# Hybrid encoder step on one core: one transfer for the rotary queries, and an order of instructions laid out by due times

## The chip, the cores and the metric

The kernel runs on one core of a Trainium2 chip. TensorE (PE) multiplies matrices, VectorE (DVE), ScalarE (ACT) and GpSimd (POOL) work on tiles, and SyncE (SP) issues every DMA of this kernel. Each engine runs its own list of instructions in a fixed order, and waits for the others by semaphores. The metric is the device time of one execution in microseconds (us), the median of several runs; less is better.

## What is computed

One step of a two-layer encoder: 2048 prompt rows (16 tiles of 128) and 64 sample rows (a 17th tile), 1024 columns. Each layer has one input projection, four groups of four heads, and one output projection:

```python
bi = branch_inputs(x, lp, jnp.arange(S))       # rms, x @ w_in, per-head rms
o_a = band_attn_prompt(bi['aq'], bi['ak'], bi['av'], lp['a_rel_bias'])
kb, vb = mla_keys(bi['ckv'], bi['krope'], lp)  # keys: 64 columns per head + 32 rotary ones
o_b = chunk_causal_attn_blocks(bi['bq'], kb, vb, MLA_SCALE)
o_c = stick_break_blocks(bi['cq'], bi['ck'], bi['cv'])
o_m = dense_attn(bi['mq'], mk, mv, HEAD_DIM ** -0.5)
y = merge(x, (o_a, o_b, o_c, o_m), bi['gates'], lp)   # rms per head, gate, @ w_out, + x
```

Group A looks at its own chunk and 8 before, B at the whole past, with a rotary part of 32 columns per head, C breaks a stick (a running product along the keys), M looks at 256 memory rows. Everything is float32.

## The kernel before

A float32 value is held as the sum of a rounded high part and a low part, and a product is made of several matmuls of such parts. For the rotary part of group B four row blocks of 32 are stacked to 128 rows: queries (high, low, high, high), keys (high, high, low, zero). `qr_stack` stores the query parts of a tile to DRAM, three blocks of them, and `load_q` reads them back for two tiles of one head, with four transfers into the tile `qr` [128 x 256], which has one buffer. `kr_stack` does the same for the keys by way of `ksbuf`.

The work is written as two streams of Python generators, which the loop at the end of `hybrid_step` interleaves. `p_stream` holds the projections: matmuls into `pp` (two PSUM banks of their own), weights split by POOL and DVE into `wh`, rows into `xh` and `xl`. `attention` goes through units, two query tiles by up to four key tiles: scores into `ps`, softmax or scan into `s` (`step`, `s1b`), transposes into `pt`, copies to `ph` (ACT the high part, DVE the low part, `s2`), the product into `ot` (`s3`), and its transpose into `ob`, from which ACT and DVE bring the result to `opark` (`s4`, `combine`). `ps`, `pt`, `ob` and all small transposes share five PSUM banks (`ps_st`). In group C a DVE scan (`TENSOR_TENSOR_SCAN` into `r`) makes the running product. `merge` normalises and gates the finished group.

What each generator issues is not sent to the engines at once. `Plan.add` records it with what it depends on, and `Plan.issue` lays all of it out in a modelled time: an operation becomes ready when the last one that it depends on has ended, plus a reserve that depends on the engine that receives it (`LAG`, in ns), and each engine that is free takes one of its ready operations, if the buffers that it opens are free in turn. Before, it takes the one that was recorded first. The order thus found is what each engine then runs; the modelled time itself is not used on the chip. Since one line (296) sends off every instruction, groups in the profile are told apart by the names of tiles.

Of the kernel before, what the change touches and what calls it, by code (L numbers as in the profile page):

```python
# [7 lines left out]
F32 = mybir.dt.float32  # L8
# [37 lines left out]
class Plan:  # L46
# [1 line left out]

    LAG = {"PE": 160, "DVE": 100, "ACT": 100, "POOL": 150, "SP": 200}

    def __init__(self):
        self.ops = []
# [129 lines left out]
    def issue(self, tc):  # L184
        import heapq
        ops, tiles = self.ops, self.tiles
        n = len(ops)
        after = [[] for _ in range(n)]
        left = [0] * n
        for i, op in enumerate(ops):  # L190
            left[i] = len(op[4])
            for j in op[4]:
                after[j].append(i)
        free, order, turn, uses = {}, {}, {}, {}
        for name, (key, k, count, bufs) in sorted(tiles.items(), key=lambda x: x[1][1]):
            free[key] = bufs
            order.setdefault(key, []).append(name)
            uses[name] = count
        rank = {x: i for names in order.values() for i, x in enumerate(names)}
        turn = {key: 0 for key in order}  # L200
        held = set()
        parked = {key: [] for key in order}
        ready = {e: [] for e in ("PE", "DVE", "ACT", "POOL", "SP")}
        clock = {e: 0.0 for e in ready}
        at = [0.0] * n
        start = [0.0] * n
        events, seq, act = [], 0, 0
        for i in range(n):
            if left[i] == 0:
                heapq.heappush(ready[ops[i][0]], i)  # L210

        def slot(i):

            for x in ops[i][5]:
                if x not in held:
                    key = tiles[x][0]
                    if free[key] <= 0 or order[key][turn[key]] != x:
                        return key
            return None

        now, done, wire = 0.0, 0, 0.0
        while done < n:
            moved = False
            for e in ready:
                while clock[e] <= now and ready[e]:
                    i = heapq.heappop(ready[e])
                    key = slot(i)
                    if key is not None:
                        parked[key].append(i)
                        continue  # L230
                    for x in ops[i][5]:
                        if x not in held:
                            k = tiles[x][0]
                            held.add(x)
                            free[k] -= 1
                            turn[k] += 1
                            if turn[k] < len(order[k]) and free[k] > 0:
                                for j in parked[k]:
                                    heapq.heappush(ready[ops[j][0]], j)
                                parked[k] = []  # L240
                    take, last = ops[i][6]
                    if e == "ACT":
                        t = self.table(ops[i][3])
                        if t and t != act:
                            act = t
                            take, last = take + 1300, last + 1300
                    if e == "SP":

                        begin = max(now + 2000, wire)
                        wire = begin + 0.004 * last  # L250
                        last = max(wire, now + 2000 + 0.0045 * last) - now + 300
                    start[i] = now
                    clock[e] = now + take
                    heapq.heappush(events, (now + take, 0, e, i))
                    heapq.heappush(events, (now + last, 1, e, i))
                    moved = True
                    break
            if moved:
                continue
            if not events:  # L260
                raise AssertionError(("plan", done, {k: (v[:3], [ops[j][0] for j in v[:3]]) for k, v in parked.items() if v}))
            now = events[0][0]
            while events and events[0][0] <= now:
                _, kind, e, i = heapq.heappop(events)
                if kind == 0:
                    if e == "PE":
                        for j in after[i]:
                            if ops[j][0] == "PE":
                                left[j] -= 1
                                if left[j] == 0:  # L270
                                    heapq.heappush(ready["PE"], j)
                    continue
                if kind == 1:
                    done += 1
                    for x in ops[i][5]:
                        uses[x] -= 1
                        if uses[x] == 0:
                            k = tiles[x][0]
                            held.discard(x)
                            free[k] += 1  # L280
                            for j in parked[k]:
                                heapq.heappush(ready[ops[j][0]], j)
                            parked[k] = []
                    for j in after[i]:
                        if e == "PE" and ops[j][0] == "PE":
                            continue
                        heapq.heappush(events, (now + (10 if ops[j][0] == e else self.LAG[ops[j][0]]), 2, e, j))
                    continue
                left[i] -= 1
                if left[i] == 0:  # L290
                    heapq.heappush(ready[ops[i][0]], i)
        self.span = now
        with tc.manual_schedule():
            for i in sorted(range(n), key=lambda i: (start[i], i)):
                op = ops[i]
                op[1](*op[2], **op[3])  # L296
# [21 lines left out]
def hybrid_step(  # L318
# [62 lines left out]
    G.memset(zrow, 0.0)  # L381
    for x in qbuf:
        V.tensor_copy(x[64:128, 1], zrow[64:128])
    ksbuf = [const.tile([128, 4, 32], F32R, name=f"ksbuf{i}") for i in range(2)]
    for x in ksbuf:
        V.tensor_copy(x[:, 3], zrow[:, 0:32])
    rot = {"q": 0, "ks": 0}

    def copy_r(dst, src):
# [15 lines left out]
    def layer_dram(l):  # L405
        d = {}
        for b, tl in enumerate(blocks):
            d["QR", b] = dt(f"qr{l}_{b}", [3, 128, len(tl) * 128])
            for g in "ABCM":
                d["Q" + g, b] = dt(f"q{g}{l}_{b}", [2, 256, len(tl) * 128])  # L410
                d["G" + g, b] = dt(f"g{g}{l}_{b}", [128, len(tl), 256])
        for g in "ABC":
            d["KV" + g] = dt(f"kv{g}{l}", [2, NH, HD, (NT + 3) // 4, 2, 512])
        for s in ("SA", "SB", "SC", "M", "SM"):
            d["KV" + s] = dt(f"kv{s}{l}", [2, NH, HD, 2, 256])
        d["KR"] = dt(f"kr{l}", [128, NT * 128])
        d["KRS"] = dt(f"krs{l}", [128, 256])
        d["Y"] = {t: dt(f"y{l}_{t}", [128, 1024]) for t in range(NT + 1)}
        D[l] = d
# [343 lines left out]
    def qr_stack(src, dst):  # L763

        pt = ps_st.tile([128, 128], F32, name="ptqr")
        T.transpose(pt, src, ident)
        kt = pj.tile([128, 2, 128], F32R, tag="qrs", name="qrs", bufs=1)
        A.copy(out=kt[:, 0], in_=pt)
        sub_r(kt[:, 1], pt, kt[:, 0])
        Y.dma_start(out=dst[0:2].rearrange("a p t -> p a t"), in_=kt.bitcast(F32))  # L770
        Y.dma_start(out=dst[2], in_=kt[:, 0].bitcast(F32))

    def v_stack(src, dst):

# [7 lines left out]
    def kr_stack(kr, dst):  # L782

        ks = ksbuf[rot["ks"] % 2]
        rot["ks"] += 1
        copy_r(ks[:, 0:2], kr.unsqueeze(1).to_broadcast([128, 2, 32]))
        sub_r(ks[:, 2], kr, ks[:, 0])
        yield
        pt = ps_st.tile([128, 128], F32, name="ptr")
        T.matmul(pt, lhsT=ks.rearrange("p a c -> p (a c)"), rhs=identr, start=True, stop=True)  # L790
# [4 lines left out]
    def small_T(src, n, tag):  # L795

        pt = ps_st.tile([128, n, 128], F32, name="pts")
        for k in range(n):
            T.transpose(pt[:, k, :], src[:, k * 128:(k + 1) * 128], ident)
        h = pj.tile([128, n, 128], F32R, tag=tag + "h", name=tag + "h", bufs=1)  # L800
        lo = pj.tile([128, n, 128], F32R, tag=tag + "l", name=tag + "l", bufs=1)
        A.copy(out=h, in_=pt)
        sub_r(lo, pt, h)
        return h, lo
# [582 lines left out]
    def group_units(l, b, g):  # L1387
# [13 lines left out]
        def load_q(p):  # L1401
# [4 lines left out]
            Y.dma_start(out=p["q"][0:64, :, 0:w].bitcast(F32), in_=src)  # L1406
            Y.dma_start(out=p["q"][64:128, 0, 0:w].bitcast(F32), in_=src[:, 0])
            if g == "B":
                p["qr"] = at.tile([128, 256], F32R, tag="qr", name="qr", bufs=1)
                for e in range(4):  # L1410
                    Y.dma_start(out=p["qr"][32 * e:32 * e + 32, 0:w].bitcast(F32),
                                      in_=d["QR", b][e % 3, h * 32:(h + 1) * 32, t0:t0 + w])

        for h in range(NH):
            start = []
# [409 lines left out]
```

## Time and profile before

| | us |
|---|---|
| median of 3 runs | 3259.86 (3255.87 to 3268.64) |
| the profiled execution's own time | 3260.81 |
| its span, first to last instruction | 3258.8 |
| PE busy | 3137.9 |
| PE loading weights | 3005.6 |
| DVE busy | 2684.0 |
| ACT busy | 1956.7 |
| POOL busy | 1509.6 |

The span is what the views of the profile divide up; the execution's own time is 2.0 us longer, and the median of the runs 0.95 us below that. PE's weight loads overlap its matmuls. SP is not in the busy times, since issuing a DMA is not counted; its issues are found in the timeline as SPq.

### The profile page before, as it was taken

What the parts mean: (1) busy time and instruction counts of PE and PEld (TensorE: products, weight loads), DVE (VectorE), ACT (ScalarE), POOL (GpSimd) and SP (SyncE); (2) the same over time, 40 slices, a digit from 0 to 9 for tenths busy, and PEclk for the clock granted to TensorE, in tenths of its full rate; (3) what the DMA queues carried; (4) which work ended last, traced back from release to release, by engine and by line L of the source; (5) the groups of instructions that cost most, each with busy time, mean ns of one, the idle gap of its engine ahead of it and who ended that gap; (6) DMA issues with size and microseconds to landing.
All of it is one profiled execution on the core that took longest, in us unless ns stands there. A gap on an engine that the chain in (4) does not pass through costs nothing. (4 is left out here: it accounts for less than half of the span.)

```text
span 3258.8 us, 75626 instructions
## 1 busy us (share of the span) xinstructions
PE 3137.9 (96%) x24486; PEld 3005.6 (92%) x24486; DVE 2684.0 (82%) x7977; ACT 1956.7 (60%) x5336; POOL 1509.6 (46%) x2353
## 2 busy tenths in 40 slices
PE   8999999999999999999999999999999999999899
PEld 7999889999999998999999889999999998998798
DVE  5687778998888789887877977899878888887984
ACT  4455656767665565565656765676646667665650
POOL 4655445665345246443434644466413544213562
PEclk9999999999999999999999999999999999999999
DMA  6755676644666766556566567754455776566545
GB/s 184 194 153 158 189 224 192 163 120 136 172 167 175 213 188 182 155 159 180 152 176 189 167 174 231 192 146 128 138 144 161 211 204 192 158 170 185 154 130 155
DMA packets 576123, 558.94 MB, mean 172 GB/s; under 512 B 70961, under 2 KB 478001, under 8 KB 575729
## 3 DMA queue, kind: packets, MB, share of 16 engines
q1 hardware_dynamic: 575728, 554.10, 60.2%
q8 instruction: 196, 3.21, 0.4%
q14 instruction: 199, 1.62, 0.2%
HBM read 378.21 MB, written 173.75 MB: 169 GB/s over the span
## 5 line engine op out<-in xcount | busy, mean ns | idle before, releaser
L296 PE MATMUL pp<-wh,xh 128*128 128x256 f32 (+1 forms) x9104 | 1804.6, 291 | 22.3 <-ACT ev L296 9.7
L296 PEld LDWEIGHTS pp<-wh,xh 128*128 128x128 f32 x9104 | 1436.3, 190 | 60.5 <-DVE wh L296 17.5
L296 PE MATMUL pp<-wh,xl 128*128 128x256 f32 (+1 forms) x4416 | 1238.2, 282 | 2.5 <-DVE xl L296 2.1
L296 PEld LDWEIGHTS pp<-wh,xl 128*128 128x128 f32 x4416 | 839.1, 190 | 7.8 <-DVE xl L296 4.5
L296 POOL TENSOR_SCALAR wh<-raw,gc 128x256 fp32r<-128x256 f32 (+1 forms) x848 | 467.5, 566 | 363.9 <-PE pp L296 268.1
L296 ACT CAST ph<-pt 128x512 fp32r<-128x512 f32 (+2 forms) x840 | 453.1, 550 | 283.5 <-PE pt L296 275.5
L296 DVE TENSOR_TENSOR ph<-pt,ph 128x512 fp32r<-128x512 f32 (+2 forms) x840 | 522.9, 633 | 119.2 <-ACT ph L296 116.0
L296 PE MATMUL ot<-ph,kv 128*128 128x256 f32 (+1 forms) x3232 | 579.3, 289 | 5.3 <-ACT os L296 1.7
L296 PE MATMUL ps<-kv,qbuf 128*128 128x256 f32 (+3 forms) x2048 | 543.4, 361 | 30.4 <-DVE r L296 8.5
L296 PE MATMUL pt<-identr,s 128*128 128x128 f32 x3056 | 504.4, 275 | 16.5 <-DVE r L296 4.8
L296 DVE SCALAR_TENSOR_TENSOR wh<-raw,gc,wh 128x256 fp32r<-128x256 f32 (+1 forms) x848 | 476.7, 597 | 22.1 <-POOL wh L296 21.5
L296 ACT ACTIVATE s<-s,nm 128x512 f32<-128x512 f32 (+4 forms) x600 | 384.3, 643 | 169.4 <-DVE nm L296 159.1
L296 PEld LDWEIGHTS ot<-ph,kv 128*128 128x128 f32 x3232 | 466.1, 190 | 18.8 <-DVE ph L296 4.4
L296 POOL TENSOR_TENSOR s<-s,r 128x512 f32<-128x512 f32 (+3 forms) x328 | 321.7, 983 | 245.0 <-DVE r L296 204.8
L296 POOL TENSOR_TENSOR st<-st,mhalf 128x4 f32<-128x4 f32 (+1 forms) x312 | 279.7, 902 | 246.1 <-DVE st L296 193.7
L296 PEld LDWEIGHTS pt<-identr,s 128*128 128x128 f32 x3056 | 356.6, 141 | 30.8 <-ACT s L296 6.6
L296 DVE TENSOR_TENSOR_SCAN r<-ps,r,one 128x512 f32<-128x512 f32 (+3 forms) x328 | 354.0, 1101 | 27.3 <-ACT ps L296 22.9
L296 PEld LDWEIGHTS ps<-kv,qbuf 128*128 128x128 f32 x2048 | 320.2, 190 | 58.2 <-DVE r L296 12.8
L296 ACT ACTIVATE ev<-pp,xst 128x256 f32<-128x256 f32 (+1 forms) x424 | 199.7, 472 | 264.0 <-PE pp L296 226.4
L296 POOL TENSOR_TENSOR mst<-mst,mhalf 128x4 f32<-128x4 f32 x136 | 138.9, 1026 | 252.9 <-DVE mst L296 244.1
L296 ACT ACTIVATE s<-ps 128x512 f32<-128x512 f32 (+3 forms) x328 | 166.4, 536 | 97.7 <-DVE ps L296 48.1
L296 DVE TENSOR_SCALAR_CACHE_REDUCE s<-ps 128x512 f32<-128x512 f32 (+1 forms) x328 | 181.6, 573 | 23.3 <-PE ps L296 22.7
(151 smaller groups left out, 4005.0 us busy)
## 6 DMA issues: line engine op xcount, KB each, us to landing
raw<-in_w_in SPq DMA_DIRECT2D x288, 256.0 KB, 3.4
kv<-kvC SPq DMA_DIRECT2D x128, 256.0 KB, 4.2
kv<-kvB SPq DMA_DIRECT2D x128, 256.0 KB, 4.2
kv<-kvA SPq DMA_DIRECT2D x96, 256.0 KB, 4.5
raw<-in_w_out SPq DMA_DIRECT2D x96, 256.0 KB, 3.7
y<-y SPq DMA_DIRECT2D x136, 128.0 KB, 2.7
xin<-y SPq DMA_DIRECT2D x64, 256.0 KB, 3.8
qC<-kt SPq DMA_DIRECT2D x34, 256.0 KB, 3.1
```

What stands on the lines that cost most here:

```text
L296: op[1](*op[2], **op[3])
```

## The change

`qr` is stored as four row blocks instead of three, the last two by one transfer from the same high part. It is read back by one transfer whose rows are interleaved: the four parts of a row lie next to each other on neighbouring partitions. The keys in `ksbuf` are interleaved in the same way. `qr` has two buffers; the two small transposes before low-rank products (`cT`, `qT`) share one pair of tiles, `sTh` and `sTl`.

In the planner, the reserves grow, and every operation gets a due time. An operation of PE or SP is due at the sum of PE's costs recorded ahead of it. One of DVE, ACT or POOL is due when its earliest reader is, less its own duration and 100 ns (and at most 100 us after its own place). A free PE takes the first recorded of those that have been ready for 300 ns, and if there is none, the first recorded. DVE and ACT take the one that is due first among those ready for 200 ns, or else among all; POOL and SP the one due first.

```diff
-    LAG = {"PE": 160, "DVE": 100, "ACT": 100, "POOL": 150, "SP": 200}
+    AGE = dict(PE=300,DVE=200,ACT=200,POOL=0,SP=0)
+    LAG = dict(PE=300,DVE=200,ACT=200,POOL=250,SP=300)
...
+        due, run = [0.0] * n, 0.0
+        for i, op in enumerate(ops):
+            due[i] = run
+            if op[0] == "PE":
+                run += op[6][0]
+        for i in range(n - 1, -1, -1):
+            if ops[i][0] in ("DVE","ACT","POOL"):
+                wait = 4000 if ops[i][0] == "SP" else ops[i][6][1] + 100
+                due[i] = min([due[i] + 100000] + [due[j] - wait for j in after[i]])
...
-                    i = heapq.heappop(ready[e])
+                    q = ready[e]
+                    if e == "PE":
+                        i = min((j for j in q if at[j] + self.AGE[e] <= now), default=q[0])
+                    else:
+                        i = min((j for j in q if at[j] + self.AGE[e] <= now), key=lambda j: due[j], default=None)
+                        if i is None:
+                            i = min(q, key=lambda j: due[j])
+                    q.remove(i)
+                    heapq.heapify(q)
...
                 if left[i] == 0:
+                    at[i] = now
                     heapq.heappush(ready[ops[i][0]], i)
...
-    ksbuf = [const.tile([128, 4, 32], F32R, name=f"ksbuf{i}") for i in range(2)]
+    ksbuf = [const.tile([128, 32, 4], F32R, name=f"ksbuf{i}") for i in range(2)]
...
-            d["QR", b] = dt(f"qr{l}_{b}", [3, 128, len(tl) * 128])
+            d["QR", b] = dt(f"qr{l}_{b}", [4, 128, len(tl) * 128])
...
-        Y.dma_start(out=dst[2], in_=kt[:, 0].bitcast(F32))
+        Y.dma_start(out=dst[2:4].rearrange("a p t -> p a t"),
+                          in_=kt[:, 0:1].bitcast(F32).to_broadcast([128, 2, 128]))
...
-        copy_r(ks[:, 0:2], kr.unsqueeze(1).to_broadcast([128, 2, 32]))
-        sub_r(ks[:, 2], kr, ks[:, 0])
+        copy_r(ks[:, :, 0:2], kr.unsqueeze(2).to_broadcast([128, 32, 2]))
+        sub_r(ks[:, :, 2], kr, ks[:, :, 0])
...
-        h = pj.tile([128, n, 128], F32R, tag=tag + "h", name=tag + "h", bufs=1)
-        lo = pj.tile([128, n, 128], F32R, tag=tag + "l", name=tag + "l", bufs=1)
+        h = pj.tile([128, n, 128], F32R, tag="sTh", name=tag + "h", bufs=1)
+        lo = pj.tile([128, n, 128], F32R, tag="sTl", name=tag + "l", bufs=1)
...
-                p["qr"] = at.tile([128, 256], F32R, tag="qr", name="qr", bufs=1)
-                for e in range(4):
-                    Y.dma_start(out=p["qr"][32 * e:32 * e + 32, 0:w].bitcast(F32),
-                                      in_=d["QR", b][e % 3, h * 32:(h + 1) * 32, t0:t0 + w])
+                p["qr"] = at.tile([128, 256], F32R, tag="qr", name="qr", bufs=2)
+
+                Y.dma_start(out=p["qr"][:, 0:w].bitcast(F32),
+                                  in_=d["QR", b][:, h * 32:(h + 1) * 32, t0:t0 + w].rearrange("e p t -> p e t"))
```

Three places show how the order moves. The first is SP's queue in group B of layer 1, block 0. `qbuf` are the queries of a pair of tiles, `qr` their rotary part; the seventh pair has `qbuf0` and `qr_7297`, the eighth `qbuf1`. Before:

```order
L296 DMA qbuf1_86<-qB1_0_165 64x2x256
L296 DMA qbuf1_86<-qB1_0_165 64x256
L296 DMA o_ckvp<-ckn_7284 128x128
L296 DMA trig_7345<-in_c_trig 128x64
L296 DMA trig_7380<-in_c_trig 128x64
L296 DMA raw_7387<-in_w_in 128x512
L296 DMA kvB1_190<-vs_7310 64x4x128 x2
L296 DMA qr_7297<-qr1_0_162 32x256 x4
```

and now:

```order
L317 DMA qbuf0_85<-qB1_0_165 64x2x256
L317 DMA qbuf0_85<-qB1_0_165 64x256
L317 DMA raw_7387<-in_w_in 128x512
L317 DMA kv_7397<-kvB1_190 64x2x256
L317 DMA qbuf1_86<-qB1_0_165 64x256
L317 DMA qr_7297<-qr1_0_162 128x1x256
L317 DMA qbuf1_86<-qB1_0_165 64x2x256
```

The seventh pair's rotary part stood behind both `qbuf1` loads of the eighth pair and five other rows; now it is one transfer between those two loads, four rows behind its own pair's.

The second is DVE in group C of layer 1, block 1. `ob_8479` is a PSUM bank whose content is added into `opark_8196`; `ph_8478` is the low part of the tile transposed just before. Before:

```order
L296 TENSOR_REDUCE st_8470<-sq_8469 128x4
L296 TENSOR_TENSOR ph_8476<-pt_8475,ph_8476 128x512
L296 SCALAR_TENSOR_TENSOR wh_8422<-raw_8401,gc_4704,wh_8422 128x256
L296 SCALAR_TENSOR_TENSOR wh_8423<-raw_8401,gc_4704,wh_8423 128x256
L296 TENSOR_SCALAR st_8470<-st_8470 128x4
L296 TENSOR_TENSOR ph_8478<-pt_8477,ph_8478 128x512
L296 TENSOR_TENSOR opark_8196<-ob_8479,opark_8196 128x2x64
L296 SCALAR_TENSOR_TENSOR wh_8445<-raw_8402,gc_4704,wh_8445 128x256
```

and now:

```order
L317 TENSOR_TENSOR nrm_8512<-ev_8511,st_8514 128x256
L317 TENSOR_TENSOR ph_8541<-pt_8540,ph_8541 128x512
L317 TENSOR_SCALAR st_8535<-st_8535 128x4
L317 TENSOR_TENSOR ph_8543<-pt_8542,ph_8543 128x512
L317 TENSOR_REDUCE st_8549<-sq_8548 128x4
L317 TENSOR_REDUCE st_8570<-sq_8569 128x4
L317 TENSOR_SCALAR st_8549<-st_8549 128x4
L317 TENSOR_TENSOR opark_8196<-ob_8479,opark_8196 128x2x64
L317 SCALAR_TENSOR_TENSOR kt_8545<-ptk_8544,qg_4706,kt_8545 128x256
L317 TENSOR_TENSOR nrm_8533<-ev_8532,st_8535 128x256
```

The addition from `ob_8479` stood right behind `ph_8478`; now it stands behind `ph_8543` and three statistics, 45 instructions further from `ph_8478`.

The third is PE in group M of layer 0, block 1. `pt_4541` is a tile being transposed, `ph_4542` its copy, `ot_4550` the product that reads it. Before, beginning behind the first transpose of `pt_4541`:

```order
L296 MATMUL ot_4539<-ph_4527,kv_4440 128x256 x3
L296 MATMUL pt_4541<-identr_79,s_4516 128x128
L296 MATMUL pt_4541<-identr_79,s_4515 128x128
L296 MATMUL pt_4541<-identr_79,s_4516 128x128
L296 MATMUL ob_4544<-identr_79,os_4521 128x128 x2
L296 MATMUL ps_4548<-kv_4485,qbuf2_87 128x256 x2
L296 MATMUL ps_4549<-kv_4485,qbuf2_87 128x256 x2
L296 MATMUL pp_4553<-wh_4376,xh_4419 128x256 x2
L296 MATMUL pp_4553<-wh_4376,xl_4420 128x256
L296 MATMUL ot_4550<-ph_4542,kv_4485 128x256
```

and now, from its last transpose:

```order
L317 MATMUL pt_4541<-identr_79,s_4516 128x128
L317 MATMUL ob_4544<-identr_79,os_4521 128x128 x2
L317 MATMUL ot_4539<-ph_4527,kv_4440 128x256 x3
L317 MATMUL ps_4548<-kv_4485,qbuf2_87 128x256 x2
L317 MATMUL ps_4549<-kv_4485,qbuf2_87 128x256 x2
L317 MATMUL pp_4553<-wh_4376,xh_4419 128x256 x2
L317 MATMUL pp_4553<-wh_4376,xl_4420 128x256
L317 MATMUL pp_4553<-wh_4377,xh_4419 128x256 x2
L317 MATMUL pp_4553<-wh_4377,xl_4420 128x256
L317 MATMUL pp_4553<-wh_4391,xh_4419 128x256 x2
L317 MATMUL pp_4553<-wh_4391,xl_4420 128x256
L317 MATMUL ot_4550<-ph_4542,kv_4485 128x256
```

Between the last transpose and the product from `ph_4542` stood nine matmuls, now eighteen: three of `ot_4539` and six projections have come between.

## Rows read from the trace of the kernel before

**Rows 1.** The page: span, and busy time of each engine with its count
```profile
span 3258.8 us, 75626 instructions
...
PE 3137.9 (96%) x24486; PEld 3005.6 (92%) x24486; DVE 2684.0 (82%) x7977; ACT 1956.7 (60%) x5336; POOL 1509.6 (46%) x2353
```

**Rows 2.** Windows: PE, PEld, DVE, ACT, POOL busy (count), then PEclk, DMA share
```profile
0.00:81.00 81.00, 66.23 (x436) 60.33 (x437) 46.44 (x160) 34.12 (x97) 37.04 (x83) 0.94 0.63 185
...
570.00:733.00 163.00, 158.58 (x1262) 152.71 (x1261) 157.44 (x366) 113.42 (x279) 109.50 (x150) 1.00 0.52 142
...
1222.00:1303.00 81.00, 73.53 (x540) 67.81 (x537) 73.58 (x154) 44.87 (x101) 51.73 (x74) 0.96 0.65 182
...
2118.00:2281.00 163.00, 158.05 (x1220) 148.97 (x1218) 157.66 (x347) 111.65 (x270) 109.87 (x151) 1.00 0.49 137
...
3014.00:3095.00 81.00, 72.21 (x517) 64.68 (x515) 78.94 (x154) 55.72 (x121) 44.50 (x60) 0.98 0.55 155
```

**Rows 3.** Waits of PE: total us, times, longest us
```profile
PE ps L296 <- DMA qr<-qr: 12.0, 10, 3.0
...
PE ptx L296 <- DMA xin<-in_x_prompt: 9.9, 4, 6.4
...
PE ps L296 <- DMA qbuf<-qM: 2.8, 3, 2.0
...
PE ot L296 <- DVE ph L296: 1.4, 5, 0.4
...
PE ot L296 <- ACT ph L296: 0.9, 2, 0.5
...
PE ps L296 <- DMA kv<-kvM: 0.5, 1, 0.5
```

**Rows 4.** Timeline of 1913.5 to 1922: start us, us, [idle before]
```profile
1915.57 3.41 SPq L296 DMA_DIRECT2D qr<-qr  x4
...
1920.55 0.45 PE L296 MATMUL ps<-kr,qr 128*128 128x128 f32 x1 [2.96 <-DMA qr<-qr]
```

**Rows 5.** Windows around that wait, columns as in rows 2
```profile
1880.00:1916.00 36.00, 34.49 (x257) 32.40 (x257) 32.66 (x130) 27.49 (x90) 20.54 (x40) 1.00 0.59 167
...
1920.00:1927.00 7.00, 6.45 (x31) 6.48 (x32) 3.92 (x19) 2.13 (x8) 2.80 (x4) 0.52 0.63 178
...
1957.00:1965.00 8.00, 6.94 (x29) 6.50 (x30) 3.93 (x12) 1.57 (x5) 3.17 (x6) 0.57 0.63 179
```

**Rows 6.** Issue time on SP: minimum, median, maximum ns
```profile
L296 SPq DMA_DIRECT2D qr<-qr x288: 302/419/1869, 125.7 to 2907.9; - x144
...
L296 SPq DMA_DIRECT2D qbuf<-qB x144: 444/600/1424, 238.8 to 2875.5; - x144
```

**Rows 7.** DMA issues: count, KB each, median us to landing
```profile
qr<-qr SPq DMA_DIRECT2D x256, 32.0 KB, 2.2
...
qbuf<-qB SPq DMA_DIRECT2D x64, 128.0 KB, 2.9
```

**Rows 8.** Timeline of PE and ACT around 1181, columns as in rows 4
```profile
1180.81 0.49 PE L296 MATMUL pt<-identr,s 128*128 128x128 f32 x3
...
1182.23 0.28 PE L296 MATMUL ot<-ph,kv 128*128 128x256 f32 x1
...
1181.34 0.59 ACT L296 CAST ph<-pt 128x512 fp32r<-128x512 f32 x1
```

**Rows 9.** Timeline of DVE around 2204, columns as in rows 4
```profile
2204.04 0.68 DVE L296 TENSOR_TENSOR ph<-pt,ph 128x512 fp32r<-128x512 f32 x1
...
2204.64 0.28 DVE L296 TENSOR_TENSOR opark<-ob,opark 128x128 f32<-128x128 f32 x1
```

**Rows 10.** Groups of the page: busy us, mean ns, idle before
```profile
L296 PE MATMUL ps<-kv,qbuf 128*128 128x256 f32 (+3 forms) x2048 | 543.4, 361 | 30.4 <-DVE r L296 8.5
...
L296 PE MATMUL pt<-identr,s 128*128 128x128 f32 x3056 | 504.4, 275 | 16.5 <-DVE r L296 4.8
...
L296 DVE TENSOR_TENSOR_SCAN r<-ps,r,one 128x512 f32<-128x512 f32 (+3 forms) x328 | 354.0, 1101 | 27.3 <-ACT ps L296 22.9
```

More of the change, by code (lines that the diff above doesn't have):

```diff
@@ L383, in hybrid_step @@
         V.tensor_copy(x[64:128, 1], zrow[64:128])
-    ksbuf = [const.tile([128, 4, 32], F32R, name=f"ksbuf{i}") for i in range(2)]
+    ksbuf = [const.tile([128, 32, 4], F32R, name=f"ksbuf{i}") for i in range(2)]
     for x in ksbuf:
-        V.tensor_copy(x[:, 3], zrow[:, 0:32])
+        V.tensor_copy(x[:, :, 3], zrow[:, 0:32])
     rot = {"q": 0, "ks": 0}
```

## The prediction

> **What bounds the kernel now.** Read the busy times first: PE is busy 3137.9 of 3258.8 us, DVE 2684.0, ACT and POOL far less [rows 1]. PE therefore bounds, and everything this change can win lies in the 3258.8 - 3137.9 = 120.9 us in which PE stands. No instruction of PE is added or removed: it has 24486 matmuls before and after. The second view is the table of windows, because the 120.9 us are not spread evenly. The first 81 us hold 81 - 66.2 = 14.8 us of it (first loads, first weights). Four stretches, 570 to 733, 1222 to 1303, 2118 to 2281 and 3014 to 3095, hold 4.4 + 7.5 + 5.0 + 8.8 = 25.7 us, and there DVE is busy 91 to 97% [rows 2]: these are the parts with group C, whose scans run on DVE, and PE waits for a full engine. The third view is PE's list of waits. Its largest row is the wait of score matmuls for `qr`, the rotary queries: 12.0 us in 10 waits. The ten other DMA rows, from 9.9 us (the inputs, mostly in the head) to 0.5 us, make 22.6 us together [rows 3]. So of 120.9 us, 14.8 are the head, 25.7 are DVE's, 12.0 are `qr`, about 12.7 are other DMAs outside the inputs, and some 56 us are many short waits for ACT, DVE and POOL, most under 1 us.
>
> **The rotary queries.** Before, `qr` has one buffer and is filled by four transfers of 32 rows; its load can go out only when the last scores of the pair before have been read. In the worst wait the four are on SP from 1915.57 for 3.41 us, and PE stands 2.96 us until 1920.55 [rows 4]. Afterwards there are two buffers and one transfer of 128 rows, and the order has `qr_7297` four rows behind the first loads of its pair, not behind all of the next pair's. Issue: four at the median 0.42 us are 1.68 us; one is not in the trace, its nearest row is `qbuf` (64 rows, also 128 KB) at a median of 0.60 us [rows 6]. Landing: 2.2 us for the 32 KB pieces, 2.9 us for the 128 KB of `qbuf` [rows 7]. From the first issue to the last landing that is 1.68 + 2.2 = 3.9 us before and 0.60 + 2.9 = 3.5 us after. The transfer itself gains only 0.4 us; what takes the wait away is the second buffer, which lets the load leave a whole pair earlier. Of the 12.0 us I take 10 as gone, bounds 0 and 12, since the next load in the same queue (`qbuf`, 2.8 us of waits) may be late in its place.
>
> Behind the two long `qr` waits PE runs at its lower clock: the granted clock is 0.52 over 1920 to 1927 and 0.57 over 1957 to 1965, between the levels 1.2 GHz (0.5) and 2.4 GHz (1.0) [rows 5]. There PE issues 31 matmuls in 7 us and 29 in 8 us; before it, in 1880 to 1916, 257 in 36 us, 7.1 per us. So 31 would take 4.4 us and 29 would take 4.1: 2.6 + 3.9 = 6.5 us lost, part of it the second wait itself. I take 5, bounds 0 and 6.5.
>
> SP is relieved too: 72 loads times 1.68 - 0.60 = 1.08 us are 78 us of queue time over the kernel. PE sees it only where it waits for a DMA whose issue is late. I take 2, bounds 0 and the 12.7 us of such waits. The store of `qr` grows by 64 KB in 34 places (one more copy of a row block) and costs SP at most the 0.2 us by which 0.60 exceeds 0.42; nothing waits for it soon. I take 0, at worst 34 x 0.2 = 7 us of a queue that has just won 78.
>
> **The small layouts.** The interleaved key buffer changes strides of 36 copies on POOL and 36 subtractions on DVE, tiles of 64 and 32 columns. No row shows such a stride. POOL is 46% busy and covers it; without that cover and at twice the mean of a DVE instruction (2684.0 us / 7977 = 0.34 us) it is 36 x 0.34 = 12 us; for a gain there is no reason. I take 0. The shared buffer for the two small transposes (`sTh`, `sTl`) can make the low-rank query wait for the key's tile. Behind the waiting ACT copy stand ACT's other evictions, behind the waiting transpose all of PE. It is used 70 times, laid out with that wait reckoned in, and PE has other matmuls then. I take 0, bounds 0 and 70 x 0.1 = 7 us, 0.1 us being less than one matmul.
>
> **The new order on PE.** The planner now reckons 300 instead of 160 ns to reach PE and prefers matmuls that have been ready for 300 ns. What that gives is seen at one place. Before, nine matmuls stand between the last transpose of `pt_4541` and the product that needs it, now 18. In the trace the transposes start at 1180.81, ACT copies from 1181.34 for 0.59 us, to 1181.93, and the product starts at 1182.23, 0.3 us later and without a wait [rows 8]. So the reserve was enough here, and doubling it wins nothing. Counted over the whole order, 85 of 840 such tiles have fewer than 12 matmuls between transpose and product before and 38 after; fewer than 18, 153 before and 174 after. Short distances were made longer, medium ones more frequent. And the waits at that product are just 1.4 + 0.9 us in all [rows 3]. The reserve can therefore win only on the 56 us of scattered short waits. Half of the shortest distances are gone, some new short ones appear: I take a quarter, 14 us, bounds 0 and two thirds, 37 us. In the four stretches of DVE I take nothing. By the order DVE has the same number of instructions between the first and last scan of a C group within 5% (347 rows and 346 in one, 297 and 295 in the last), so a full engine stays full.
>
> **The new order on DVE.** DVE, ACT and POOL now take, of what is ready, what is due first. A result is due when its reader is, but the due time knows nothing of the PSUM bank that it frees. The addition into `opark` reads a bank `ob` and is needed only at the group's end, so it is put off. In the trace it starts at 2204.64, straight behind the `ph` at 2204.04 [rows 9]; in the new order 45 other DVE instructions stand between these two, some 45 x 0.34 = 15 us. Counted over the order, none of 384 `ob` banks was emptied behind a later `pt` bank; now 96 are, 25 of them behind three or more. All these share five banks. What waits behind a missing bank is PE's whole queue, but the projections (`pp`) have two other banks to fill in with, so I take a loss of 5 us, bounds 0 and 53 (below, the second rival).
>
> **The sum.** -10 - 5 - 2 - 14 + 5 = -26 us against the profiled execution's own 3260.8 us (span 3258.8 and 2.0 around it): 3234.8. The median of the runs is 3259.9, 0.9 lower, so 3234 us, 0.8% faster. Its own range goes from 12 + 6 + 2 + 22 = 42 us won (`qr` whole, the clock, SP, a reserve between my value and its bound) to 10 us won (`qr` and clock less the banks, no reserve): 3218 to 3250. A change under 0.5% (16 us) cannot be told from none here.
>
> **Rivals.** First, nothing measurable. The PE rows show that the reserves were sufficient and that C stays with DVE; then only `qr` (10) and the clock (5) go, and parked banks take 10 back: 3260.8 - 5 = 3255.8, or 3255. Against it: 56 us of short waits are a large target. The Trainium skill, Perfetto Trace Analysis, DMA Optimizations, says that splitting a transfer can let some of it start sooner when the DMA engines are mostly idle, which speaks for four pieces against one; by that rule the `qr` term too would be about nothing. The rows above (3.9 against 3.5 us) do not bear it out, but the merged transfer itself is in no row.
>
> Second, slower, by parked banks. With `ob` parked, fewer than five banks turn over, and PE's next `ps` or `pt` has no bank until DVE gets to the addition. Price: DVE's longest instruction, the scan, takes 1101 ns on average [rows 10]; if half of the 96 late additions make PE wait one scan, 48 x 1.1 = 53 us: 3260.8 - 10 - 5 - 2 + 53 = 3296.8, or 3296. It decides once PE's idle before `ps` and `pt`, now 30.4 + 16.5 = 47 us [rows 10], doubles. For it: DVE is full just where additions are put off. Against it: what DVE does first is then what PE needs, and the order was laid out with the five banks counted. The Trainium skill (the same page, Matmuls) wants independent groups of matmuls to rotate through different banks so that one is emptied while the next is filled; the order of before does that, the new one less, and no run here shows its price.
>
> Third, more than I think: the reserves take two thirds of the 56 us (37), `qr` all 12, the clock 6, SP's relief 9: -64, 3196.
>
> **Chances and range.** Forecast 0.52, of it 0.04 above 3243.5 and thus within 0.5%; no measurable change 0.22; slower by banks 0.16; more than thought 0.10. Faster 0.48 + 0.10 = 0.58, same 0.04 + 0.22 = 0.26, slower 0.16. The range 3200 to 3272 holds the forecast, the first rival, and about half of the third.
>
> **What the new profile would show.** Right: `DMA qr<-qr` gone from PE's waits, no lower clock in the 1900s, PE's idle near 95 us, the four C stretches as before, idle before `ps` not larger. Wrong: the idle in front of `ps` and `pt` behind DVE grows while `qr` is gone (second rival), or PE's short waits keep their sum (first).

## The result, and the profile after

The changed kernel takes 3226.13 us (median of 4 runs, 3224.78 to 3227.39) against 3259.52 us before: a ratio of 0.9897, 95% interval 0.9883 to 0.9911, so 33 us or 1.0% faster. The profiled execution took 3226.14 us. Its page, the span and the busy time of each engine with its count of instructions:

```profile
span 3224.4 us, 75446 instructions
...
PE 3122.8 (97%) x24486; PEld 3000.2 (93%) x24486; DVE 2645.8 (82%) x7977; ACT 1957.0 (61%) x5336; POOL 1514.3 (47%) x2353
```

Beside [rows 1], the span is 34.4 us shorter with the same 24486 matmuls. PE's idle time fell by 19.3 us, from 120.9 to 101.6, and its busy time by 15.1. That busy time can shrink is seen in the trace: the matmuls overlap. One of 256 columns lasts 281 ns by the profile, which models its end, and the next one starts 118 ns after it (medians over the changed kernel). A pause counts as idle only from that end on, and what lies before it, like a matmul drawn out at the lower clock, counts as busy. PE's list of waits (total us, times, longest us) says where the idle time went:

```profile
PE ptx L317 <- DMA xin<-in_x_prompt: 8.9, 3, 6.9
PE ps L317 <- DVE r L317: 7.1, 15, 1.4
PE pp L317 <- ACT ev L317: 7.1, 5, 4.4
...
PE ot L317 <- ACT ph L317: 4.0, 3, 2.7
PE ps L317 <- DMA kv<-kvC: 3.4, 2, 3.2
...
PE ot L317 <- DVE ph L317: 1.8, 3, 1.3
...
PE ps L317 <- DMA qbuf<-qM: 0.4, 1, 0.4
```

The row `DMA qr<-qr` of [rows 3], 12.0 us, is gone, and `qbuf<-qM` went from 2.8 to 0.4. Summed over the whole list, PE's waits for DMAs fell from 36.0 to 16.3 us. Waits for DVE, ACT and POOL together did not fall: 68.9 before, 74.1 after. On balance the idle time won was thus DMA waiting. The sum of the other waits moves with the order by itself: in two kernels below that differ from this one by a mere reshuffle it is 71.9 (`e10`) and 64.7 (`e11`).

Counted from start to start of the matmuls, beyond the usual spacing of their shape, pauses of over 1 us shrank by 18 us in all, those of 150 ns to 1 us by 11, and the rest, matmuls at the lower clock among it, by 6. As for the clock, the trace's record has 57.7 us at the lower level before and 44.8 after, which is worth about half the difference, 6 us. This holds for the two profiled executions alone. Over all runs the mean granted clock is no higher: 0.993 on average in 4 runs of the changed kernel, 0.994 in 35 of the kernel before.

The groups that answer to [rows 10] (busy us, mean ns, idle before and what ended most of it) show `ps` with less idle time in front of it than before, 18.9 us against 30.4, and `pt` the same:

```profile
L317 PE MATMUL ps<-kv,qbuf 128*128 128x256 f32 (+3 forms) x2048 | 546.0, 360 | 18.9 <-DVE r L317 7.1
L317 PE MATMUL pt<-identr,s 128*128 128x128 f32 x3056 | 499.7, 274 | 16.1 <-ACT s L317 5.9
```

The new load itself, from the view of the tile `qr` (duration on SP in ns, minimum, median, maximum):

```profile
L317 SPq DMA_DIRECT2D qr<-qr x72: 532/556/1867, 125.2 to 2856.3; - x72
```

It takes 0.556 us of the queue and lands 3.0 us after its issue; 0.60 and 2.9 were assumed from [rows 6, 7]. All `qr` loads together held SP for 46.1 us, against 136.1 before (sums over the trace).

The place of [rows 4] looks like this now, in the timeline (start us, us, idle before in brackets):

```profile
1914.47 0.56 SPq L317 DMA_DIRECT2D qr<-qr  x1
...
1916.30 0.62 PE L317 MATMUL pt<-identr,s 128*128 128x128 f32 x4
1919.61 0.39 PE L317 MATMUL ot<-ph,kv 128*128 128x256 f32 x1 [2.69 <-ACT ph L317]
1920.69 0.50 PE L317 MATMUL pp<-wh,xh 128*128 128x256 f32 x2 [0.70 <-ACT ev L317]
```

The load leaves in a sixth of the time and nothing waits for it, but a little later PE stands for 2.69 us, now put down to ACT. The windows that answer to [rows 5] (busy us and count of PE, PEld, DVE, ACT, POOL, then PE's clock) show what followed:

```profile
1880.00:1916.00 36.00, 33.84 (x259) 31.94 (x258) 32.92 (x131) 24.91 (x86) 20.30 (x35) 1.00 0.76 220
1920.00:1927.00 7.00, 6.31 (x41) 6.31 (x42) 4.23 (x19) 3.38 (x13) 0.69 (x3) 0.76 1.04 278
1957.00:1965.00 8.00, 8.00 (x66) 7.73 (x65) 7.08 (x27) 5.87 (x21) 3.84 (x5) 1.00 0.78 217
```

The second spell at the lower clock is gone (66 matmuls in 8 us where there were 29). The first is shorter, not gone: after the 2.69 us pause the granted clock averages 0.76 over those 7 us, a mixture of 1.2 and 2.4 GHz.

Last, the stretches of group C. The two kernels reach them at different times, so they are set by the first and last scan of each. Before:

```profile
2131.00:2315.00 184.00, 178.31 (x1367) 167.65 (x1366) 177.35 (x350) 124.11 (x293) 120.86 (x168) 1.00 0.44 123
2989.00:3151.00 162.00, 150.21 (x1111) 139.01 (x1110) 154.82 (x299) 110.70 (x241) 91.12 (x121) 0.98 0.49 135
```

and after:

```profile
2108.00:2288.00 180.00, 176.79 (x1368) 167.92 (x1368) 171.76 (x349) 123.45 (x289) 118.58 (x166) 1.00 0.46 127
2959.00:3121.00 162.00, 152.80 (x1138) 140.60 (x1136) 151.74 (x300) 108.56 (x236) 92.38 (x126) 0.99 0.50 139
```

The first passes 1368 matmuls in 180 us instead of 1367 in 184; the second passes 1138 instead of 1111 in the same 162. DVE is a little less full (95 and 94% for 96 and 96%). By these counts, which take matmuls of all sizes alike, the two gained some 4 us each; the other two pass as many matmuls per us as before, within 1%.

### The profile page after: what moved, and what is told of

It reads as the page before. It is cut to its first block, busy times and chain, and to the rows that moved or that the text cites. A ratio compares the mean times of both kernels' runs of the same rounds, so it can differ in the third digit from the quotient of the medians.

```text
span 3224.4 us, 75446 instructions
## 1 busy us (share of the span) xinstructions
PE 3122.8 (97%) x24486; PEld 3000.2 (93%) x24486; DVE 2645.8 (82%) x7977; ACT 1957.0 (61%) x5336; POOL 1514.3 (47%) x2353
## 5 line engine op out<-in xcount | busy, mean ns | idle before, releaser
L317 POOL TENSOR_SCALAR wh<-raw,gc 128x256 fp32r<-128x256 f32 (+1 forms) x848 | 476.9, 577 | 389.8 <-PE pp L317 287.4
L317 PE MATMUL ps<-kv,qbuf 128*128 128x256 f32 (+3 forms) x2048 | 546.0, 360 | 18.9 <-DVE r L317 7.1
L317 PEld LDWEIGHTS ps<-kv,qbuf 128*128 128x128 f32 x2048 | 321.1, 191 | 46.1 <-DVE r L317 12.8
L317 ACT ACTIVATE s<-ps 128x512 f32<-128x512 f32 (+3 forms) x328 | 168.4, 536 | 101.1 <-DVE ps L317 46.1
```

## The experiments

All times are ratios to the kernel before on the same chip, with 95% intervals; 0.1% is 3.3 us.

### Which half?

`e1` is the changed kernel with the planner of before; `e2` is the kernel before with the new planner.

```diff
 e1: class Plan            (all of it as before; qr, ksbuf, sT* as changed)
 e2: qr, ksbuf, sT*        (as before; class Plan as changed)
```

> The rotary-query edits alone (four row blocks, one transfer, two buffers, shared transposed tiles), the planner as before. Theory of the prediction, by terms: the wait for qr (10 to 12 us) and the lower clock behind it (5) go, so 3242 to 3247 us, and DMA qr leaves PE's list of waits. Rival, the planner does it all: 3255 to 3262, the wait for qr comes back as another wait in the same place.

> The planner's edits alone (reserves, due times, ages), the rotary queries as before with four transfers and one buffer. Theory of the prediction: reserves 14 less banks 5, so about 3250 us, with the wait for qr still 8 to 12 us in PE's list. Rival, the planner does it all: 3226 to 3232. Second rival, the two halves need each other: 3255 or more.

`e1`: 3247.11 us, 0.9965 [0.9952, 0.9978], about 11 us. `e2`: 3238.04 us, 0.9935 [0.9923, 0.9947], about 21 us. The wait for `qr` is gone from PE's list in `e1` and still 10.8 us in `e2`. The two add up to the whole change (32 of 33 us), so the halves neither need nor hinder each other, and two thirds belong to the planner, more than the expectation gave it.

### Which part of the planner?

`e3` and `e4` split the planner on top of `e1`: only the larger reserves, or only the new choice.

```diff
 e3, on e1:
-    LAG = {"PE": 160, "DVE": 100, "ACT": 100, "POOL": 150, "SP": 200}
+    LAG = dict(PE=300,DVE=200,ACT=200,POOL=250,SP=300)
 e4, on the changed kernel:
-    LAG = dict(PE=300,DVE=200,ACT=200,POOL=250,SP=300)
+    LAG = {"PE": 160, "DVE": 100, "ACT": 100, "POOL": 150, "SP": 200}
```

> Rotary-query edits and the larger reserves, but each engine takes the first recorded of what is ready, as before. If the reserves are what wins in the planner: 3226 to 3234 us, or below 3226 if putting off the additions into opark costs what was predicted (5 us). If the due times win: as with the rotary queries alone, about 3243.

> Rotary-query edits and the choice by due times and age, but the old, smaller reserves. If the reserves win in the planner: 3243 to 3250 us, at or above the rotary queries alone. If the choice wins: 3226 to 3232 us.

`e3`: 3241.03 us, 0.9947 [0.9934, 0.9960]. `e4`: 3229.09 us, 0.9910 [0.9897, 0.9923]. Against `e1`'s 0.9965 the reserves alone win some 6 us, the choice alone some 18, both together 22.

### What in the choice?

`e7` leaves the due times to DVE, ACT, POOL and SP but lets PE take what was recorded first. `e8` does the reverse.

```diff
 e7:
                     if e == "PE":
-                        i = min((j for j in q if at[j] + self.AGE[e] <= now), default=q[0])
+                        i = q[0]
 e8:
+                    elif e != "PE":
+                        i = q[0]
```

> The changed kernel, but PE takes the first recorded of its ready matmuls, without the age of 300 ns. If PE's age carries the choice's gain (14 us over the smaller set of edits): 3236 to 3241 us. If the due times on DVE, ACT and POOL carry it: 3225 to 3230.

> The changed kernel, but DVE, ACT, POOL and SP take the first recorded of what is ready; PE keeps its age. If the due times carry the gain: 3236 to 3241 us, as with reserves alone. If PE's age carries it: 3225 to 3230, or below that by up to 5 us if putting off the additions into opark has a price, since here none is put off.

`e7`: 3222.66 us, 0.9893 [0.9878, 0.9909]. `e8`: 3224.11 us, 0.9891 [0.9877, 0.9904]. Neither lost anything, where the expectations had one of the two carry the gain. With both taken away the kernel is `e3` (0.9947), which loses 0.5%. Either rule by itself is enough on top of the reserves: PE's age wins some 18 us (`e8` over `e3`), the due times also some 18 (`e7` over `e3`), both together no more than one.

### How much does an order by itself move?

`e10` and `e11` add or take 10 ns to every reserve. This says nothing about the hardware; it only makes the planner lay out another order by the same rules.

```diff
-    LAG = dict(PE=300,DVE=200,ACT=200,POOL=250,SP=300)
+    LAG = dict(PE=310,DVE=210,ACT=210,POOL=260,SP=310)   # e10; e11: 290, 190, 190, 240, 290
```

> The changed kernel with all reserves 10 ns larger (310, 210, 210, 260, 310), which has no meaning of its own: it shows how much a mere reshuffle of the order moves the time. If little: 3224 to 3230 us. If reshuffles are worth as much as the terms of a few us that the other runs differ by: up to 6 us away on either side.

> The changed kernel with all reserves 10 ns smaller (290, 190, 190, 240, 290), the second sample of a mere reshuffle: as the first, 3224 to 3230 us if the order's fine grain does not matter, else up to 6 us away.

`e10`: 3223.34 us, 0.9895 [0.9880, 0.9910]. `e11`: 3217.71 us, 0.9878 [0.9864, 0.9891]. Beside 0.9897 an order laid out anew differs by up to 0.2%, 6 us, in these two draws. Differences of that size between the kernels here, such as those of `e7` and `e8` to the changed kernel, are not to be read, and the 6 us of `e3` barely.

### What do parked banks cost?

`e9` is the changed kernel in which whatever touches an `ob` bank is due at its own place, so that the bank is emptied at once.

```diff
-                due[i] = min([due[i] + 100000] + [due[j] - wait for j in after[i]])
+                own = 0 if any(x.startswith("ob") for x in ops[i][5]) else 100000
+                due[i] = min([due[i] + own] + [due[j] - wait for j in after[i]])
```

> The changed kernel, but an operation that reads an ob bank is due at its own place in the record, so that none of the 384 banks is emptied behind a later pt bank (96 were). The prediction put 5 us on parked banks, bounds 0 and 53: 3215 to 3222 us if they cost that or more. Rival, putting them off is free or a help, since DVE does first what PE waits for: 3224 to 3232.

`e9`: 3207.25 us (3203.14 to 3209.81), 0.9849 [0.9835, 0.9862]. It is the fastest kernel of this study: 1.5% faster than before, 10 us faster than `e11` and 16 us faster than `e10`, which were timed beside it. The 10 us are the safer figure: the mean granted clock of `e11`'s runs is that of `e9`'s, 0.995, and `e10`'s is 0.993. By the order, none of 384 banks is emptied behind a later `pt` bank, against 96 in the changed kernel. The trace shows it at the bank of [rows 9] (`ob_8479`). In the changed kernel PE fills it at 2172.41; ACT and DVE each empty half:

```profile
2172.41 0.40 PE L317 MATMUL ob<-identr,os 128*128 128x128 f32 x2
...
2172.85 0.27 ACT L317 COPY opark<-ob 128x128 f32<-128x128 f32 x1 [0.78 <-PE ob L317]
...
2197.63 0.28 DVE L317 TENSOR_TENSOR opark<-ob,opark 128x128 f32<-128x128 f32 x1
```

and in `e9`:

```profile
2162.89 0.44 PE L318 MATMUL ob<-identr,os 128*128 128x128 f32 x2
...
2163.36 0.27 ACT L318 COPY opark<-ob 128x128 f32<-128x128 f32 x1 [0.54 <-PE ob L318]
...
2165.18 0.26 DVE L318 TENSOR_TENSOR opark<-ob,opark 128x128 f32<-128x128 f32 x1
```

ACT is prompt in both. DVE's half is held for 25 us in the changed kernel and 2 us in `e9`. Over all 384 banks, from the end of PE's last transpose to the end of the last read, the mean is 2.1 us before, 4.8 after (the longest 60) and 1.5 in `e9`. It is 2.2 in `e8`, which has no due times on DVE and ACT, and 4.9 in `e7`, which has: the parked banks come with the due times. That bears on the two rules above. Due times laid on top of PE's age win nothing as they are (0.9891 to 0.9897), but some 14 us once banks are left out of them (0.9891 to 0.9849). The reading that fits is that the parked banks take back what the due times win. Since `e9` empties the banks sooner than even the kernel before did, its 10 to 16 us are a price of parked banks from above; the part that the change itself added may be smaller. Its page:

```profile
span 3204.2 us, 75344 instructions
...
PE 3111.0 (97%) x24486; PEld 2995.0 (93%) x24486; DVE 2648.3 (83%) x7977; ACT 1956.6 (61%) x5336; POOL 1514.9 (47%) x2353
```

and its groups:

```profile
L318 PE MATMUL ps<-kv,qbuf 128*128 128x256 f32 (+3 forms) x2048 | 547.1, 360 | 17.0 <-DVE r L318 5.2 <-DMA kv<-kvC 2.6 <-DVE ph L318 2.5
L318 PE MATMUL pt<-identr,s 128*128 128x128 f32 x3056 | 501.3, 274 | 14.1 <-ACT s L318 5.4 <-DVE opark L318 2.2 <-DVE r L318 1.7
```

PE idles 93.2 us instead of 101.6, and 3.9 us of that lie before `ps` and `pt`. But `e11` idles 93.2 us too, in a span of 3218.5; against it, `e9` gains within PE's busy time. And the waits that name the release of a bank, `DVE opark` in PE's list, do not get shorter. In the changed kernel there is one, in `e9` there are two rows:

```profile
PE ps L317 <- DVE opark L317: 0.2, 1, 0.2
```

```profile
PE pt L318 <- DVE opark L318: 2.2, 2, 1.7
PE ps L318 <- DVE opark L318: 0.8, 2, 0.5
```

So it is shown that emptying the banks at once wins 10 to 16 us. That PE would otherwise stand waiting for a bank is not: the profile speaks against it. A price paid in the order, which the planner lays out around banks that are taken, or an effect of the earlier additions on the work behind them, would fit; no run tells these apart.

### Two buffers or one transfer?

The prediction said that the second buffer takes the wait for `qr` away and that the single transfer itself wins next to nothing. `e5` is the kernel before with two buffers and its four transfers (and the shared `sTh`, `sTl`). `e6` is `e1`, so with one transfer, but into one buffer; against the kernel before it also has the interleaved keys, the fourth stored row block and the shared tiles.

```diff
 e5, on the kernel before:
-                p["qr"] = at.tile([128, 256], F32R, tag="qr", name="qr", bufs=1)
+                p["qr"] = at.tile([128, 256], F32R, tag="qr", name="qr", bufs=2)
 e6, on e1:
-                p["qr"] = at.tile([128, 256], F32R, tag="qr", name="qr", bufs=2)
+                p["qr"] = at.tile([128, 256], F32R, tag="qr", name="qr", bufs=1)
```

> Planner and transfers as before (four of 32 rows), but two buffers for qr, with the shared transposed tiles that make room. The prediction says that the second buffer, not the single transfer, takes the wait away: as the rotary-query edits alone, 0.9965 of before, within 0.15%. Rival, the single transfer does it: 0.999 to 1.001, with the wait for qr still in PE's list.

> Planner as before, one interleaved transfer, but one buffer for qr. The prediction: by 3.9 against 3.5 us to land, most of the wait for qr stays, 0.998 to 1.001. Rival, the issue time on SP is what counts: 0.9955 to 0.997 and the wait gone from PE's list.

`e5`: 3253.79 us, 0.9985 [0.9976, 0.9994]. `e6`: 3242.45 us, 0.9947 [0.9934, 0.9961]. PE's waits in `e5` hold no `qr` any more; the largest for DMAs:

```profile
PE ptx L296 <- DMA xin<-in_x_prompt: 7.9, 3, 6.8
...
PE ptk L296 <- DMA ev<-in_ca_k: 3.0, 1, 3.0
...
PE ptx L296 <- DMA xin<-y: 2.5, 4, 0.8
...
PE ps L296 <- DMA kv<-kvC: 2.0, 1, 2.0
```

In `e6` the wait for `qr` is shorter but there:

```profile
PE ps L296 <- DMA qr<-qr: 3.4, 7, 0.9
```

So the buffer takes away the wait and wins 5 us, no more than an order by itself moves; the transfer, with the edits that come with it, leaves 3.4 of 12.0 us of the wait and wins about 17. Both results lie outside what was expected of them. In `e5`, waits for all DMAs fell by 12.2 us, and those for ACT rose by 5.8 (19.2 to 25.0); its clock gave nothing back (58.0 us at the lower level, 57.7 before). A wait's row is not its price. The clock is not what `e6` won by either: its runs have the mean granted clock of the kernel before, 0.994. In `e6`, SP issues `qr` for 43.5 us in all instead of 136.1; the four transfers of a load hold the queue for 1.7 us, the one for 0.56, and what is queued behind them leaves that much sooner. From the first issue of a load to its last landing it is 3.1 us on average, 4.2 before. That the shorter queue is why it wins is the reading that fits; the next run was to show it. As for the order of the two, `e6` and `e1` (0.9965) lie within what an order alone moves, so the second buffer adds nothing that can be measured once the transfer is single.

The Trainium skill (Perfetto Trace Analysis, DMA Optimizations) says that splitting a transfer can help while DMA engines are mostly idle. Here they are 60% busy over the span before, so the rule's condition does not hold, and it says nothing against the 0.5% that the kernel with the merged transfer won.

### The count of transfers by itself

`e12` is `e6` with the load in four transfers again, each of a quarter of the rows.

```diff
-                Y.dma_start(out=p["qr"][:, 0:w].bitcast(F32),
-                                  in_=d["QR", b][:, h * 32:(h + 1) * 32, t0:t0 + w].rearrange("e p t -> p e t"))
+                for e in range(4):
+                    Y.dma_start(out=p["qr"][32 * e:32 * e + 32, 0:w].bitcast(F32),
+                                in_=d["QR", b][:, h * 32 + 8 * e:h * 32 + 8 * e + 8, t0:t0 + w].rearrange("e p t -> p e t"))
```

> Planner as before, one buffer, interleaved rows, but loaded by four transfers of 32 partitions, so that only the number of transfers differs from the run with one transfer and one buffer (0.9947 of before). If the issues on SP are what cost: 0.998 to 1.001, with the wait for qr back at 8 us or more. If the interleaved layout or chance in the order made the gain: 0.994 to 0.996.

`e12`: 3293.91 us, 1.0116 [1.0097, 1.0134]: slower than before. The tile's view and PE's waits say why it is no clean test:

```profile
L296 SPq DMA_DIRECT2D qr<-qr x288: 644/684/1612, 125.4 to 2943.6; - x144
```

```profile
PE ps L296 <- DMA qr<-qr: 21.7, 21, 4.2
```

A quarter made of 8 rows by 4 parts takes 684 ns of the queue, where a plain block of 32 rows took 419 and the whole load 556. Two things changed at once, the count and the shape. It does show that a kernel with longer issues and later `qr` loads is slower (2.8 us of SP per load, 21.7 us of waits, 1.7% slower than `e6`), and that with the interleaved layout and four transfers nothing was won. The time that SP issues over the whole kernel goes with the ratios: 1798 us before, 1792 in `e5` (0.9985), 1704 in `e6` (0.9947), 1870 in `e12` (1.0116). `e1`, with 1707 us and 0.9965, is off that line by as much as an order alone moves. This supports the reading and does not prove it.

The Trainium skill (DMA: Bandwidth & Descriptors, Rules for kernel authors) says that an outermost dimension below 16 confines a DMA to at most as many engines; the quarters have 8. The trace agrees in so far as each of the 288 quarters leaves 9 updates on its semaphore, where every other DMA that SP issues leaves 16. Which engines they used no view here shows.

## Why the prediction was right, and where it was not

The time came out at 3226, where 3234 was forecast with 3218 to 3250. The sign and size were right, the terms were not: two were too small and one too large. The rotary half gave 11 us where 17 were put, PE's order 24 for 14, DVE's order about nothing for a loss of 5. That the sum came within 8 us is in part luck. The premise that all there is to win lies in PE's 120.9 idle us was wrong too: 15 of 34 us came out of its busy time.

**The rotary queries (10, with clock 5 and SP 2: 17 us).** Alone they gave 11 us (`e1`, 7 to 16 by its interval). The row of the wait did go, and SP won 90 us of queue time where 78 were reckoned. The step that failed is "what takes the wait away is the second buffer": true of the wait, not of the time. The buffer alone gave 5 us, the transfer with its layout about 17. The 0.4 us by which the transfer was reckoned to land sooner measured 1.1 us on average. What the loads behind it in the same queue gain was costed at 2 us and is the likelier seat of the rest, which no run shows.

**The clock (5 us).** Of the two spells in the 1900s one is gone, the other shorter, since a pause for ACT came where the pause for `qr` was. In the two profiled executions PE won about 6 us by the clock. Over all runs the mean granted clock did not rise (0.993 after, 0.994 before), so this term is not borne out as a gain of the change.

**The new order on PE (14 us).** Right in sign, too small, and for another reason. This term joined the reserves and PE's age; together they give 24 us (`e8` over `e1`), of which the reserves are 6 (`e3` over `e1`) and the age 18. They were to shorten the scattered waits for DVE, ACT and POOL, of which a quarter was taken; in the changed kernel those did not fall at all (68.9 to 74.1 us), and `e10` and `e11` lie on both sides of the old sum. The reading of [rows 8], that the old reserve was enough there, was borne out; what the age does was not seen in it.

**The new order on DVE (a loss of 5 us).** The banks are parked as counted, and emptying them at once wins 10 to 16 us, some of which the kernel before may have paid already. The wait that was to carry the price, PE's queue behind a missing bank, is not seen (0.2 us for `opark`). The step that failed is the one that let this be the only effect of due times. They win about as much elsewhere (18 us as `e7` over `e3`, 14 as `e9` over `e8`), so that on top of the other edits they come to nothing instead of 5 us lost.

**The four stretches (0 us).** By the counts above two of them won some 4 us each. "A full engine stays full" was read from the count of DVE's rows between two scans; about the same count finished sooner.

**The rivals.** The first (nothing, 3255) is out. The second asked for idle time before `ps` and `pt` to double from 47 us; it fell to 35. The third (3196) is out for this kernel, though `e9` with 3207 comes near it by a way that it did not name. Of the signs: the `qr` row gone, yes; no lower clock in the 1900s, in part; PE idle near 95 us, 101.6; stretches as before, no, a little better; idle before `ps` not larger, yes.

**Left open.** Why PE's age adds nothing where due times stand, parked banks included (`e7` to the changed kernel); which pauses of PE the choice shortens; by what path the parked banks cost time; how the 17 us of the single transfer divide between the wait, the queue and the order.

## What to carry to other kernels

The rows of a list of waits are places, not prices: taking 12 us of `qr` waits away by a buffer returned 5, and a load that holds its queue for a third of the time returned more than the wait that was listed, by a path that is not shown. When instructions are ordered by when their result is needed, give the release of a scarce buffer a due time too; here two lines that did so were worth a third to a half as much as the whole change. And before reading a difference between two laid-out orders, move the planner's numbers by a little and see what that alone does.

## What the runs showed of the hardware

SP's time to issue a DMA depends on its shape more than on its size: 419 ns for a plain block of 32 rows (32 KB), 556 ns for 128 interleaved rows (128 KB), 684 ns for 32 interleaved rows (32 KB, medians). A load whose source has 8 rows outermost left 9 updates on its semaphore instead of 16. DVE's busy time fell with the new choice, from 2684.0 to 2645.8 us with the same 7977 instructions (2681.0 in `e1`, 2655.3 in `e4`), and their durations by 28 us in sum; why was not tried.
